# Gate projections of the mLSTM heads by seven block products, with head outputs kept in memory and gate rows made by scans

## The chip, the cores and the metric

The kernel runs on one core of one Trainium2 chip. The metric is the device time of one execution in microseconds (us); less is better. The kernel before takes 914.85 us, the median of three executions (914.61 to 915.66).

## The reference

Two residual layers work on x, 512 rows of 1024 fp32 values. Each computes x + norm(mixer(norm(x))) with a root-mean-square norm on either side. The even layer's mixer has four mLSTM heads (A) and eight stick-breaking attention heads (B); the odd layer's mixer is a trailing-window mean. What matters here, shortened:

```python
u = rmsnorm(x, pre_g) @ w_in                       # 512x1024 @ 1024x9224
qa, ka, va, oa, za, ia, fa, qb, kb, vb, zb = split_cols(u, sizes)
ig, lf = ia + b_i, log_sigmoid(fa + b_f)           # two gates per A head and row
ha = mlstm(silu(conv(qa)), silu(conv(ka)), va, ig, lf)
ya = head_norm(sigmoid(oa) * ha, hn_g) * silu(za)
yb = stick_breaking(qb, kb, vb) * silu(zb)
x = x + rmsnorm(concat([ya, yb]) @ w_out, post_g)  # 512x2048 @ 2048x1024
```

`oa` and `za` are the gate projections of the A heads: 512x1024 times 1024x256 for each head and each of the two. The mLSTM needs, for each head, the running sum of `lf` along the rows and a running maximum of `ig` minus that sum.

## The kernel before

Every fp32 factor of a large product is held as a high and a low part of type fp32r. `split` (L70) makes them: ScalarE copies the value to the high part, VectorE subtracts that to get the low part. `mm3` (L93) then issues three matmuls: high by high, high by low, low by high. `halves` (L86) splits a weight tile, and there are four buffers for the parts (`wh`, `wl`) and two for the fp32 weights (`w32`), which SyncE's DMA queue loads 1 MB at a time (`load`, L78).

`prenorm` (L161) normalises 128 rows, transposes them on TensorE into a bank of PSUM and splits them into `hTh` and `hTl`, the activations with the 1024 features on partitions (eight tiles) and the 512 rows beside. With `keep` (L184) it also stores the fp32 value, which only the second layer uses. `project2` (L196) computes 256 output columns as two groups of 8 x 3 matmuls of 128x512, so 48 matmuls; `raw2` (L350) copies the result out of PSUM (L354).

The even layer runs eight B heads in four pairs (`heads_b`, `stick_pair`, then `raw2` for zb and `close`, L493), then the four A heads in turn: q and k (`project2`, `conv_silu`), v (`values`), the scores `s` and the numerator `num` (`mlstm`, L357), the gates oa and za by `raw2`, and `mlstm_out` (L391). In `mlstm`, the decay weights `w` (ScalarE) are multiplied with the scores on VectorE (L370) and split into `ph` and `pl`, which TensorE multiplies with v. The A heads' gate rows come from `gate_rows` (L248), placed with the third pair: transposes `ips` and `fps`, the logarithm, seven doubling steps for the sum (L277), four transposes into `cps` (L289), seven doubling steps for the maximum, and a store to memory that each head reads back as `bc`.

The head outputs go to `y32` (L101), 32 KB in each partition that lives through the whole kernel. Before it is filled, its space holds the first layer's input tiles (`xt0`, `xs0`, `gain0`) and the gate rows. `out_steps` (L548) walks over the 16 tiles of y in pairs: `y_split`, the out-projection's weights, and 12 matmuls per tile and half of the rows. The first half uses the order `EVEN` (tiles 8 to 15, then 0 to 7), the second `EVEN2`.

The odd layer already uses `strassen2` (L688) for six of its eight z projections. It computes the 1024x256 by 512 product as seven block products instead of eight: sums of weight blocks (`ws`, four VectorE additions), four `halves`, 7 x 4 x 3 = 84 matmuls of 128x256 on sums of activation blocks (`d3`, `d1`, `n2`, `t4`, made by `hidden_sums`, L672), and additions that put the pieces together (`pt`, L715 to L725). Its three PSUM accumulators `psa`, `psb`, `pse` take banks of the tags `pj` (two), `xa` and `xb` (one each). In the A heads `xa` also holds the denominator `den`, and `xb` the mean `mn`.

The program order is not the code's order. A tile framework takes the code as a graph and orders each engine's instructions by a simulated timeline; each engine, and each DMA queue with its issuing engine, then runs its list in order.

Of the kernel before, what the change touches and what calls it, by code (L numbers as in the profile page):

```python
# [36 lines left out]
def body(nc, tc, x, pre_g, post_g, w_in, conv, b_i, b_f, hn_g, w_out, w_in_c, pool_w,  # L37
# [6 lines left out]
    with base as base, psum as psum, dram as dram:  # L44
# [24 lines left out]

        def split(src, hi, lo):  # L70
            A.activation(hi, src, AF.Copy)  # L71
            V.tensor_tensor(lo, src, hi.bitcast(F32), op=ALU.subtract)  # L72
# [28 lines left out]
        y32 = base.tile([P, 16, S], F32, name="y32")  # L101
        yflat = y32.rearrange("p a n -> p (a n)")
        cT = base.tile([P, NB, HA], F32, name="cT")


        xt0 = [yflat[:, i * D:(i + 1) * D] for i in range(4)]
        xs0 = [yflat[:, (4 + i) * D:(5 + i) * D] for i in range(2)]
        gain0 = yflat[:, 6 * D:7 * D]
        xr = x[0].rearrange("(a p) d -> p a d", p=P)
# [51 lines left out]
        def prenorm(xt, xs, tt, gain, name, parts=1, keep=None):  # L161
# [10 lines left out]
            for half in range(2):  # L172
# [10 lines left out]
                if keep is not None:  # L183
                    A.activation(keep[:, half * 4:half * 4 + 4], tp, AF.Copy)  # L184
# [17 lines left out]
        with tc.tile_pool(name="att", bufs=1) as at:  # L202

            def qkt(name): return at.tile([P, S], F32R, tag="qk", bufs=11, name=name)
            def tmp(name): return at.tile([P, S], F32, tag="tmp", bufs=7, name=name)
            def phi(name): return at.tile([P, S], F32R, tag="phi", bufs=4, name=name)
            def plo(name): return at.tile([P, S], F32R, tag="plo", bufs=4, name=name)
            def ozt(name): return at.tile([P, S], F32, tag="oz", bufs=7, name=name)

            def vtile(name):  # L210
                return (at.tile([P, NB, 256], F32R, tag="vh", bufs=2, name=f"vh_{name}"),
                        at.tile([P, NB, 256], F32R, tag="vl", bufs=2, name=f"vl_{name}"))


            v01 = [vtile(f"vb{h}") for h in range(2)]
            w01 = []

            def values01(tt):
                ps = pj(f"psv01_{tt}")
                ts = slice(tt * P, tt * P + P)  # L220
                for k in range(8):
                    wh, wl = w01[k // 2]
                    mm3(ps, (hTh[:, k, ts], hTl[:, k, ts]), (wh[:, k % 2], wl[:, k % 2]),
                        k == 0, k == 7)
                for h in range(2):
                    split(ps[:, 256 * h:256 * h + 256], v01[h][0][:, tt], v01[h][1][:, tt])

            for tt in range(NB):
                prenorm(xt0[tt], xs0[tt % 2], tt, gain0, f"p0{tt}", 1 if tt else 2)
                if tt == 0:  # L230
                    for i in range(2):
                        if i:
                            nc.sync.dma_start(xt0[1], xr[:, 1])
                        w = load(lambda t: [(nc.sync, t[:, 2 * j:2 * j + 2],
                                             w_in[0, 512 * i + 256 * j:512 * i + 256 * j + 256,
                                                  VB:VB + 512]) for j in range(2)], 4, 512, f"v01{i}")
                        w01.extend(halves(w[:, 2 * j:2 * j + 2], f"v01{i}{j}") for j in range(2))
                    for t in range(2, NB):
                        nc.sync.dma_start(xt0[t], xr[:, t])
# [602 lines left out]
```

## Time and profile before

| | us |
|---|---|
| median of three executions | 914.85 |
| the profiled execution | 914.12 |
| its span, first to last instruction | 912.2 |
| ScalarE busy | 485.6 |
| VectorE busy | 570.6 |
| GpSimd busy | 77.3 |

PE is TensorE, DVE is VectorE, ACT is ScalarE, POOL is GpSimd and SP is SyncE, in all rows that follow. Of a row of instruction groups, the name left of the arrow is the tile written, the names right of it are those read; the last numbers are the total busy time, the mean of one in ns, and the idle time before them on the same engine with what ended it. Matmuls are pipelined: one starts long before the one ahead of it ends, so what a matmul costs PE is the distance from its start to the next start, not its listed duration.

### The profile page before, as it was taken

The numbers are of one execution on the slowest core, as the hardware profiler recorded it, in microseconds if no ns is written. First come the engines' busy times: TensorE is split into PE (matmuls) and PEld (weight loads), VectorE is DVE, ScalarE is ACT, GpSimd is POOL, SyncE is SP. The second block draws the span as 40 slices with busy tenths as digits, with TensorE's granted clock in tenths as the row PEclk, the third lists the DMA queues.
The fourth block names the chain that finished last, engine by engine and source line by source line (L and its number), as shares of the span: only waits on it lengthen the run. The fifth ranks groups of instructions, "written<-read, shape, count | busy, mean of one in ns | idle before, by whom it ended". The sixth has DMA issues, their size and how long they took to land.

```text
span 912.2 us, 12027 instructions
## 1 busy us (share of the span) xinstructions
PE 897.8 (98%) x4669; PEld 764.9 (84%) x4669; DVE 570.6 (63%) x847; ACT 485.6 (53%) x814; POOL 77.3 (8%) x221
## 2 busy tenths in 40 slices
PE   7999999999999999999999999999999999999996
PEld 6788889889988888898898887898889898988885
DVE  5435546567876685664775738578484867957442
ACT  6426676766668464564565527574244343455331
POOL 2001101001101201001001000005020110200000
PEclk8999999999999999999999999999999999999999
DMA  8231322222222421333312456623223233146321
GB/s 301 79 107 47 94 71 69 70 70 60 81 93 87 133 93 66 113 94 127 98 49 91 139 185 210 205 93 119 66 92 117 71 127 105 51 160 231 132 96 46
DMA packets 67128, 98.91 MB, mean 108 GB/s; under 512 B 2848, under 2 KB 54136, under 8 KB 67072
## 3 DMA queue, kind: packets, MB, share of 16 engines
q1 hardware_dynamic: 65888, 98.08, 32.7%
q8 instruction: 36, 0.59, 0.2%
q10 hardware_dynamic: 1184, 0.08, 0.1%
q14 instruction: 20, 0.16, 0.1%
HBM read 96.02 MB, written 2.13 MB: 108 GB/s over the span
## 4 chain that ended last, share of the span: by engine, by line
PE 96%; DVE 1%; ACT 1%; DMA 1%; issue 0%; SPq 0%; DVEq 0%; POOL 0%; POOLq 0%; ACTq 0%
PE op L540 10%; PE oq L540 10%; PE ps_qa L97 3%; PE ps_qa L95 3%; PE ps_qa L96 3%; PE ps_p L95 3%; PE ps_p L97 3%; PE ps_p L96 3%; PE psv_va L95 2%; PE psv_va L97 2%; PE psv_va L96 2%; PE ps_zb L95 2%; PE mx L96 2%; PE mx L97 2%; PE mx L95 2%; PE ps_oa L96 2%
## 5 line engine op out<-in xcount | busy, mean ns | idle before, releaser
L95 PE MATMUL ps_p<-hTh,wh_p 128*128 128x512 f32 (+1 forms) x160 | 55.8, 350 | 0.4 <-ACT p L748 0.4
L96 PE MATMUL ps_p<-hTl,wh_p 128*128 128x512 f32 (+1 forms) x160 | 55.9, 350 | 0.2 <-DVE hTl L72 0.2
L97 PE MATMUL ps_p<-hTh,wl_p 128*128 128x512 f32 (+1 forms) x160 | 55.7, 348 | 0.0
L97 PE MATMUL ps_qa<-hTh,wl_qa 128*128 128x512 f32 x128 | 50.3, 393 | 0.0
L95 PE MATMUL ps_qa<-hTh,wh_qa 128*128 128x512 f32 x128 | 50.2, 393 | 0.0
L96 PE MATMUL ps_qa<-hTl,wh_qa 128*128 128x512 f32 x128 | 50.2, 392 | 0.0
L72 DVE TENSOR_TENSOR wl_wo_e<-w_wo_e,wh_wo_e 128x1024 fp32r<-128x1024 f32 x28 | 34.3, 1232 | 23.3 <-ACT wh_wo_e L71 23.2
L71 ACT ACTIVATE wh_wo_e<-w_wo_e 128x1024 fp32r<-128x1024 f32 x28 | 29.4, 1058 | 29.0 <-DMA w_wo_e<-in_w_out_ab 12.3
L71 ACT ACTIVATE wh_p<-w_p 128x1024 fp32r<-128x1024 f32 x16 | 16.9, 1058 | 51.1 <-issue 31.9
L540 PE MATMUL op<-wh_wo_e,yl_e 128*128 128x512 f32 x120 | 39.1, 396 | 0.0
L540 PE MATMUL op<-wl_wo_e,yh_e 128*128 128x512 f32 x120 | 39.1, 396 | 0.0
L540 PE MATMUL op<-wh_wo_e,yh_e 128*128 128x512 f32 x120 | 37.8, 395 | 0.0
L67 ACT ACT_TABLE_LOAD x28 | 35.9, 1283 | 1.3 <-PEq L827 0.8
L97 PE MATMUL psv_va<-wh_va,hTl 128*128 128x256 f32 x128 | 36.1, 282 | 0.0
L95 PE MATMUL psv_va<-wh_va,hTh 128*128 128x256 f32 x128 | 36.1, 282 | 0.0
L96 PE MATMUL psv_va<-wl_va,hTh 128*128 128x256 f32 x128 | 36.1, 282 | 0.0
L320 DVE SCALAR_TENSOR_TENSOR cv<-u,vecs,cv 128x511 f32<-128x511 f32 (+2 forms) x48 | 35.4, 748 | 0.4
L95 PEld LDWEIGHTS ps_p<-hTh,wh_p 128*128 128x128 f32 x160 | 30.1, 189 | 4.7 <-ACT p L748 0.6
L96 PEld LDWEIGHTS ps_p<-hTl,wh_p 128*128 128x128 f32 x160 | 30.2, 189 | 4.3 <-DVE hTl L72 0.4
L97 PEld LDWEIGHTS ps_p<-hTh,wl_p 128*128 128x128 f32 x160 | 30.2, 189 | 4.1
L72 DVE TENSOR_TENSOR wl_wo_o<-w_wo_o,wh_wo_o 128x1024 fp32r<-128x1024 f32 x20 | 24.3, 1223 | 12.5 <-ACT wh_wo_o L71 12.4
L767 POOL TENSOR_TENSOR p<-p,invc 128x1 f32<-128x1 f32 (+3 forms) x16 | 18.4, 1151 | 157.8 <-DVE p L762 157.7
(379 smaller groups left out, 2826.9 us busy)
## 6 DMA issues: line engine op xcount, KB each, us to landing
w_wo_e<-in_w_out_ab SPq DMA_DIRECT2D x14, 1024.0 KB, 4.8
w_wo_o<-in_w_out_c SPq DMA_DIRECT2D x12, 1024.0 KB, 4.8
w_qa<-in_w_in_ab SPq DMA_DIRECT2D x8, 1024.0 KB, 4.9
w_p<-in_w_in_c SPq DMA_DIRECT2D x8, 1024.0 KB, 5.3
w_z<-in_w_in_c SPq DMA_DIRECT2D x8, 1024.0 KB, 5.3
w_qb<-in_w_in_ab SPq DMA_DIRECT2D x4, 1024.0 KB
w_kb<-in_w_in_ab SPq DMA_DIRECT2D x4, 1024.0 KB, 5.2
w_zb<-in_w_in_ab SPq DMA_DIRECT2D x4, 1024.0 KB, 5.1
```

The source lines that it names most:

```text
L67: link(A.preload_act_table_set(TABLE[func]))
L71: A.activation(hi, src, AF.Copy)
L72: V.tensor_tensor(lo, src, hi.bitcast(F32), op=ALU.subtract)
L95: T.matmul(dst, lhsT=ah, rhs=bh, start=first, stop=False, **kw)
L96: T.matmul(dst, lhsT=ah, rhs=bl, start=False, stop=False, **kw)
L97: T.matmul(dst, lhsT=al, rhs=bh, start=False, stop=last, **kw)
L320: V.scalar_tensor_tensor(acc[:, j:], u[:, :S - j], cw(3 - j, c), acc[:, j:], op0=ALU.mult, op1=ALU.add)
L540: T.matmul(ps[a][n], lhsT=l[:, ta], rhs=r[:, 0, n * 512:n * 512 + 512], start=(first and l is yh and r is wh), stop=(last and l is yl))
L767: G.tensor_tensor(sm[:, :e], sm[:, :e], invc[:, :e], op=ALU.mult)
```

## The change

- **Gates.** Each A head's oa and za come from `strassen2` instead of `raw2`: eight calls. `strassen2` now takes its pool and its activation sums; the buffers for `pt` are three instead of four.
- **Activation sums.** The first layer's `prenorm` keeps fp32 transposes (`h32`, eight ScalarE copies of 128x512), and `activation_sums` makes d3, d1, n2, t4 from them (eight VectorE operations of 128x512, four splits of 128x1024) after the first pair's projections; `behind` fixes their place on VectorE.
- **Head outputs.** `close` and `mlstm_out` write their product over z, and GpSimd's DMA queue stores it to `ydr` in memory (16 stores of 256 KB). `out_steps` reads pairs of half tiles back (`yt`, 16 reads of 256 KB on SyncE's queue), one pair ahead. The first pair is read during the last head (`yh_early`); for the second half `soon`, one of the two `w32` buffers, holds two early reads.
- **Gate rows.** Each row of doubling steps becomes four scan instructions of 4x128; the rows take a `bc` buffer and three `oz` tiles. The denominator's floor is computed before the gates (`mlstm_den`).
- **Space.** `y32` exists only in the odd layer; the first layer's input tiles have a pool of their own that closes before the sums' pool opens.

The core of the diff, with the indentation of the moved blocks left as it is in the new file; `strassen2` and the odd layer's `hidden_sums` moved up unchanged but for the arguments and the `part` buffers:

```diff
             wh, wl = (t[:, :a * n].rearrange("p (a n) -> p a n", a=a) for t in (into or whl(name)))
-            split(w, wh, wl)
+            low[name] = split(w, wh, wl)
...
-        y32 = base.tile([P, 16, S], F32, name="y32")
+        ydr = dram.tile([P, 16, S], F32, name="ydr")
...
+        def activation_sums(pool, quarter, tile, order=()):
...
+                for (cs, p), (_, q) in zip(x, y):
+                    if n in ("d3", "d1"):
+                        i = V.tensor_tensor(raw[:, :, cs], p, q, op=ALU.subtract)
+                    else:
+                        i = V.scalar_tensor_tensor(raw[:, :, cs], p, -1.0, q, op0=ALU.mult,
+                                                   op1=ALU.subtract)
+                    if order:
+                        behind(i, order[len(made)])
...
+                split(raw, *hs[n])
...
+        def strassen2(pool, hs, src, name, dsts, silu=False):
...
+            def part(i): return pool.tile([P, 256], F32, tag="part", bufs=3, name=f"pt{i}_{name}")
...
-                prenorm(xt0[tt], xs0[tt % 2], tt, gain0, f"p0{tt}", 1 if tt else 2)
+            prenorm(xt0[tt], xs0[tt % 2], tt, gain0, f"p0{tt}", 1 if tt else 2, h32[tt].__getitem__)
...
-                def scan(buf, op):
-                    cur = 0
-                    for sh in (1, 2, 4, 8, 16, 32, 64):
-                        V.tensor_tensor(buf[1 - cur][:, :, 64:], buf[cur][:, :, 64:],
-                                        buf[cur][:, :, 64 - sh:192 - sh], op=op)
...
+            for B in range(NB):
+                cs = slice(B * P, B * P + P)
+                V.tensor_tensor_scan(b[:, cs], unit, f0[:, cs], 0.0, ALU.mult, ALU.add)
...
+                V.tensor_tensor_scan(mx[:, cs], g[:, cs], g[:, cs], -1e30, ALU.max, ALU.max)
...
-                    V.tensor_tensor(y32[:, c], us[j], z[j], op=ALU.mult)
+                V.tensor_tensor(z[j], us[j], z[j], op=ALU.mult)
+                G.dma_start(ydr[:, c], z[j])
...
-                    V.tensor_tensor(y32[:, 8 + self.h], self.o, z, op=ALU.mult)
+                V.tensor_tensor(z, self.o, z, op=ALU.mult)
+                G.dma_start(ydr[:, 8 + self.h], z)
...
+        def y_back(tile):
+            def src(half, c):
+                t = tile(f"yt{half}{c}").rearrange("p (a n) -> p a n", a=2)
+                nc.sync.dma_start(t, ydr[:, c:c + 2, half * 256:half * 256 + 256])
+                return t
+            return src
...
-                o = raw2(OA + 256 * h, f"oa{h}")
-                z = raw2(ZA + 256 * h, f"za{h}")
-                mlstm_out(h, num, den, bc, o, z)
+            dd = mlstm_den(h, den, bc)
+            o, z = ([ozt(f"r_{n}{h}_{j}") for j in range(2)] for n in ("oa", "za"))
+            if h == HA - 1:
+                ready = y_split(y_back(tmp)(0, EVEN[0]), (qkt("yh_early"), qkt("yl_early")))
+            for t, off, n in ((o, OA, "oa"), (z, ZA, "za")):
+                strassen2(at, hs, w_in[0, :, off + 256 * h:off + 256 * h + 256], f"{n}{h}", t)
+            mlstm_out(h, num, dd, o, z)
...
+        soon = base.tile([P, 8 * WIDE // 4], F32, tag="w32", bufs=2, name="soon")
+        early = [y_back(lambda n, i=i: soon[:, i * S:i * S + S])(1, EVEN2[2 * i]) for i in range(2)]
```

**How the order moves.** Each row is one instruction, or several alike with their count: line, operation, tile written and tiles read, shape. The numbers at the ends of names tell buffers apart.

First place: TensorE in the third A head, between the scores `s` and the numerator `num`. Before, the last scores of the second block are followed by 26 matmuls of the oa projection:

```order
L97 MATMUL s_3917<-h_5_3671,l_5_3756 128x384
L95 MATMUL ps_oa_0_3990<-hTh,wh_oa_0_3991 128x512
L96 MATMUL ps_oa_0_3990<-hTl,wh_oa_0_3991 128x512
...
L95 MATMUL ps_oa_1_4021<-hTh,wh_oa_1_4022 128x512
L96 MATMUL ps_oa_1_4021<-hTl,wh_oa_1_4022 128x512
L95 MATMUL s_3938<-h_4_3630,h_4_3714 128x256
L96 MATMUL s_3938<-l_4_3631,h_4_3714 128x256
L97 MATMUL s_3938<-h_4_3630,l_4_3715 128x256
L95 MATMUL num_3893<-ph_3907,vh_va_3773 128x512
```

Now the same place holds the twelve narrow matmuls of the third and fourth blocks' scores and twelve of the product on `n2`:

```order
L105 MATMUL s_4196<-h_5_3971,l_5_4056 128x512
L105 MATMUL s_4217<-h_5_3971,l_5_4056 128x384
L103 MATMUL s_4238<-h_4_3930,h_4_4014 128x256
...
L105 MATMUL s_4259<-h_5_3971,l_5_4056 128x256
L103 MATMUL psa_oa_4320<-n2h,wh_oa_b 128x256
...
L105 MATMUL psa_oa_4320<-n2h,wl_oa_b 128x256
L103 MATMUL num_4193<-ph_4207,vh_va_4073 128x512
L103 MATMUL num_4194<-ph_4207,vh_va_4073 128x512
L104 MATMUL num_4193<-pl_4208,vh_va_4073 128x512
```

The work between a block's scores and its numerator has become shorter on TensorE.

Second place: VectorE in the gate rows, from the transposed gates `fps` to the four additions (L363) that the transposes into `cps` need. Before:

```order
L263 TENSOR_SCALAR y_65<-fps,gb 4x512
L72 TENSOR_TENSOR vl_vb_2040<-psv_vb_2078,vh_vb_2039 128x256
L271 SCALAR_TENSOR_TENSOR y_65<-y_65 4x4x128
L277 TENSOR_TENSOR y_65<-y_65 4x4x128 x2
L493 TENSOR_TENSOR y_65<-o_1528,r_zb_0_1802 128x512
L277 TENSOR_TENSOR y_65<-y_65 4x4x128
L493 TENSOR_TENSOR y_65<-o_1529,r_zb_1_1833 128x512
```

Now:

```order
L350 TENSOR_SCALAR gr_1897<-fps,gb 4x512
L80 TENSOR_TENSOR vl_vb_2098<-psv_vb_2136,vh_vb_2097 128x256
L354 SCALAR_TENSOR_TENSOR gr_1897<-gr_1897,gr 4x512
L358 SCALAR_TENSOR_TENSOR gr_1899<-ones,gr_1897 4x128 x4
L378 TENSOR_TENSOR tot<-gr_1899 4x1
L360 TENSOR_TENSOR gr_1897<-gr_1898,gr_1899 4x512
L577 TENSOR_TENSOR r_zb_0_1864<-o_1590,r_zb_0_1864 128x512
L577 TENSOR_TENSOR r_zb_1_1895<-o_1591,r_zb_1_1895 128x512
L363 TENSOR_SCALAR gr_1898<-gr_1897,gr_1899 4x128 x4
```

The four scans (L358) stand where the doubling steps began, and on TensorE the `cps` transposes have moved up with them: 67 rows after `fps` instead of 111.

Third place: SyncE's DMA queue at the change from the first half of the out-projection to the second. Before, weights follow weights:

```order
L83 DMA w_wo_e_4945<-in_w_out_ab 128x2x1024
L83 DMA w_wo_e_4983<-in_w_out_ab 128x2x1024
L83 DMA w_wo_e_5171<-in_w_out_ab 128x2x1024
L83 DMA w_wo_e_5209<-in_w_out_ab 128x2x1024
L630 DMA g_post_5026<-in_post_norm_g 128x1024
```

Now:

```order
L637 DMA yt_5455<-ydr 128x2x256
L91 DMA w_wo_e_5421<-in_w_out_ab 128x2x1024
L91 DMA w_wo_e_5461<-in_w_out_ab 128x2x1024
L91 DMA w_wo_e_5501<-in_w_out_ab 128x2x1024
L637 DMA yt_5495<-ydr 128x2x256
L91 DMA w_wo_e_5539<-in_w_out_ab 128x2x1024
L637 DMA soon<-ydr 128x2x256 x2
L91 DMA w_wo_e_5736<-in_w_out_ab 128x2x1024
```

The read `yt_5495` fetches the last A head's output and so stands behind that head's two stores; a weight load, the two reads into `soon` and another weight load stand behind it.

More of the change, by code (lines that the diff above doesn't have):

```diff
@@ L1 @@
+from contextlib import ExitStack
 import concourse.bass as bass
@@ L183, in prenorm @@
                 if keep is not None:
-                    A.activation(keep[:, half * 4:half * 4 + 4], tp, AF.Copy)
+                    A.activation(keep(half), tp, AF.Copy)
         def col_load(src, name):
@@ new lines, in body, with values01 @@
+        v01 = [vtile(f"vb{h}") for h in range(2)]
+        w01, h32 = [], []
+        def values01(tt):
+            ps = pj(f"psv01_{tt}")
+            ts = slice(tt * P, tt * P + P)
+            for k in range(8):
+                wh, wl = w01[k // 2]
+                mm3(ps, (hTh[:, k, ts], hTl[:, k, ts]), (wh[:, k % 2], wl[:, k % 2]),
+                    k == 0, k == 7)
+            for h in range(2):
+                low["v01"] = split(ps[:, 256 * h:256 * h + 256], v01[h][0][:, tt], v01[h][1][:, tt])
@@ new lines, in stick_pair, with first, second @@
+        def stick_pair(pair, tags):
+            def first(si, t):
+                for s, tag in zip(pair, t):
+                    s.scores(si, tag)
+                for s in pair:
+                    s.soft_exp(si)
+                for s in pair:
+                    s.soft_ln(si)
+            def second(si):
+                for s in pair:
+                    s.sums(si)
+                for s in pair:
+                    s.weigh(si)
+            for si in range(NB - 1, -1, -1):
+                first(si, tags[si % 2])
+                if si < NB - 1:
+                    second(si + 1)
+            second(0)
@@ new lines, in out_tile @@
+        def out_tile(steps, ps, a):
+            ends = steps[-1][2]
+            for group in ([(s, (n,)) for n in range(2) for s in steps] if ends else
+                          [(s, (0, 1)) for s in steps]):
+                ((wh, wl), (yh, yl), last, first), ns = group
+                ta = slice(a * P, a * P + P)
+                for l, r in ((yh, wh), (yh, wl), (yl, wh)):
+                    for n in ns:
+                        T.matmul(ps[a][n], lhsT=l[:, ta], rhs=r[:, 0, n * 512:n * 512 + 512],
+                                 start=(first and l is yh and r is wh), stop=(last and l is yl))
@@ L638, in ytiles, with back @@
                         od.tile([P, S], F32R, tag="plo", bufs=5, name=f"yl_{n}"))
-            ready = y_split(1, EVEN2[0], ytiles("first"), "e")
+            load_y = y_back(lambda n: od.tile([P, S], F32, tag="sz", bufs=4, name=n))
+            def back(half, c): return early[1] if c == EVEN2[2] else load_y(half, c)
+            ready = y_split(early[0], ytiles("first"))
             xn = od.tile([P, NB, D], F32, name="xn")
+            y32 = od.tile([P, 16, S], F32, name="y32")
             gpo, gpr = gains(post_g[0], "g_post0"), gains(pre_g[1], "g_pre1")
```

813 lines of the change are left out of this document (392 added, 421 removed).

## The prediction

> **What bounds the kernel now.** I read the page's busy times first, then the chain that ended last, then what TensorE waited for, then windows of single stages. All rows are of the profile of before.
>
> ```profile
> span 912.2 us, 12027 instructions
> PE 897.8 (98%) x4669; PEld 764.9 (84%) x4669; DVE 570.6 (63%) x847; ACT 485.6 (53%) x814; POOL 77.3 (8%) x221
> PE 96%; DVE 1%; ACT 1%; DMA 1%; issue 0%; SPq 0%; DVEq 0%; POOL 0%; POOLq 0%; ACTq 0%
> PE tp_p L179 <- DVE y L174: 3.2, 1, 3.2
> PE warm L119 <- POOL ident masks.py:199: 1.6, 1, 1.6
> PE op L540 <- POOL p L740: 0.8, 1, 0.8
> ```
>
> TensorE is busy for 98% of the span and carries 96% of the chain. Its longest waits (total, times, longest) are 3.2 and 1.6 us, both in the opening; the next is 0.8 us. The windows (length; busy us of PE, PEld, DVE, ACT, POOL with counts; granted clock; DMA share; GB/s) say where the slack of the others lies:
>
> ```profile
> 0.00:30.00 30.00, 24.75 (x111) 19.77 (x112) 16.97 (x29) 17.14 (x31) 5.13 (x37) 0.89 0.65 229
> 30.00:60.00 30.00, 30.00 (x134) 24.52 (x133) 12.59 (x15) 10.88 (x15) 0.00 (x0) 1.00 0.33 106
> 410.00:470.00 60.00, 60.00 (x310) 51.27 (x309) 38.62 (x53) 31.07 (x48) 4.00 (x9) 1.00 0.31 104
> 680.00:740.00 60.00, 60.00 (x370) 53.70 (x369) 42.94 (x59) 26.02 (x41) 7.62 (x24) 1.00 0.33 106
> ```
>
> 410 to 470 is most of an A head: TensorE full, VectorE 64%. 680 to 740 is the odd layer with three calls of the seven-product form: TensorE full too, VectorE at 72%. So the kernel ends when TensorE has worked off its list, and a change counts by the matmuls it removes and by the waits it brings.
>
> **The change part by part.** First the price of a matmul, by the distance of starts:
>
> ```profile
> 409.93 0.39 PE L95 MATMUL ps_oa<-hTh,wh_oa 128*128 128x512 f32 x1
> 415.96 0.28 PE L95 MATMUL s<-h,h 128*128 128x256 f32 x1
> 689.72 0.28 PE L96 MATMUL psa_z<-n2l,wh_z_b 128*128 128x256 f32 x1
> 694.24 0.40 PE L95 MATMUL mx<-pph,wh_pw 128*128 128x512 f32 x1
> ```
>
> From 409.93 to 415.96 stand 26 matmuls of 128x512: 6.03 / 26 = 0.232 us each. From 689.72 to 694.24 stand 38 of 128x256, of four products: 4.52 / 38 = 0.119 us each. A projection was 48 x 0.232 = 11.13 us and becomes 84 x 0.119 = 9.99 us. It saves 1.14 us, and eight of them **9.1 us**. The other matmul groups keep their shapes and counts.
>
> *VectorE and ScalarE in an A head.* The new work has its rows in the odd layer, with the same shapes:
>
> ```profile
> L72 DVE TENSOR_TENSOR wl_oa<-w_oa,wh_oa 128x1024 fp32r<-128x1024 f32 x8 | 9.8, 1223 | 6.5 <-ACT wh_oa L71 6.5
> L72 DVE TENSOR_TENSOR wl_z_c<-ws_z,wh_z_c 128x1024 fp32r<-128x1024 f32 x6 | 7.3, 1222 | 2.2 <-ACT wh_z_c L71 1.6 <-PE psa_z L97 0.5
> L72 DVE TENSOR_TENSOR wl_z_d<-w_z,wh_z_d 128x512 fp32r<-128x512 f32 x6 | 4.1, 687 | 0.1
> L696 DVE TENSOR_TENSOR ws_z<-w_z 128x512 f32<-128x512 f32 x6 | 4.2, 692 | 15.0 <-DMA w_z<-in_w_in_c 15.0
> L725 DVE TENSOR_TENSOR sz<-pse_z,pt_z 128x256 f32<-128x256 f32 x6 | 2.5, 422 | 10.6 <-PE pse_z L97 10.6
> L71 ACT ACTIVATE wh_oa<-w_oa 128x1024 fp32r<-128x1024 f32 x8 | 8.5, 1062 | 16.5 <-PE ps_qa L96 16.5
> L715 ACT ACTIVATE pt_z<-psa_z 128x256 f32<-128x256 f32 x6 | 2.3, 376 | 0.5 <-PE psa_z L97 0.3
> L354 ACT ACTIVATE r_oa<-ps_oa 128x512 f32<-128x512 f32 x8 | 4.6, 579 | 0.0
> ```
>
> A call adds on VectorE four weight sums (4 x 0.69), one whole and one half low part more (1.22 + 0.69) and three pieces (3 x 0.42): 5.9 us, so 11.9 us in a head with two calls. ScalarE gets 1.5 high parts (1.6) and four copies of 128x256 (1.5) and loses two of 128x512 (1.2): +1.9 us a call. The window of 410 to 470 says 38.6 of 60, so 41.5 us of VectorE in a head of 64.4. With the new work it is at most 53.4 us in a head of 64.4 - 2.3 = 62.1: 86%. That is below TensorE, but the cover of each single chain shrinks. The shortest is the one from scores to numerator that the order shows:
>
> ```profile
> 410.25 1.15 DVE L370 SCALAR_TENSOR_TENSOR w<-s,w 128x512 f32<-128x512 f32 x2
> 411.32 1.22 DVE L72 TENSOR_TENSOR wl_za<-w_za,wh_za 128x1024 fp32r<-128x1024 f32 x1
> 412.45 0.69 DVE L72 TENSOR_TENSOR pl<-w,ph 128x512 fp32r<-128x512 f32 x1
> 417.38 0.39 PE L96 MATMUL num<-pl,vh_va 128*128 128x512 f32 x1
> ```
>
> Before, `pl` was ready at 413.14 and TensorE wanted it at 417.38: 4.2 us to spare. Now TensorE has, from the start of the first block's last score to the first `num` on `pl`: one matmul of 128x512, one of 128x384 (0.17), 24 of 128x256 and two `num` of 128x512, so 0.23 + 0.17 + 2.86 + 0.46 = 3.7 us. The chain needs 0.4 us until that score has ended, the 2.9 us that it took before from `w` to the end of `pl`, and 0.3 us more for the rows that now stand between (a value part, one more `w`, half a weight part: about 1.5 us where 1.1 stood): 3.6 to 4.2 us. The wait is 0 to 0.5 us a head. I take 0.25, so **+1.0 us** for four heads. What queues behind it: `num` heads TensorE's list, so all of TensorE waits.
>
> *Gate rows.* After the change the transposes into `cps` stand about 8.2 us of matmuls behind `fps` (before about 18), and VectorE must have finished by then:
>
> ```profile
> 212.83 0.27 PE L261 MATMUL fps<-ident,gates 128*4 128x128 f32 x1
> 216.75 0.68 DVE L271 SCALAR_TENSOR_TENSOR y<-y 4x512 f32<-4x512 f32 x1
> L277 DVE TENSOR_TENSOR y<-y 4x512 f32<-4x512 f32 x14 | 9.4, 675 | 0.2
> L286 DVE TENSOR_SCALAR y<-y 4x128 f32<-4x128 f32 x4 | 0.9, 270 | 0.0
> L412 DVE RECIPROCAL dd<-dd 128x512 f32<-128x512 f32 x4 | 13.4, 3354 | 2.1 <-ACT dd L68 2.1
> ```
>
> From `fps` to the end of L271 before the sums: 217.43 - 212.83 = 4.6 us. Behind it come four scans, a tiny addition (0.1), one operation of 4x512 (0.6), two head products (1.2) and four additions of 4x128 (0.9): 7.4 us and four scans. No scan stands in the trace. By the additions of 4x128 one costs 0.22 us in a row, by an operation that does one element at a time like the reciprocal 3354 / 4 = 0.84 us. So cps is ready 8.3 to 10.8 us after `fps`, a wait of 0.1 to 2.6 us, once. I take 0.3 us for a scan, nearest the row of its own shape: **+0.4 us**. The VectorE time saved is about 14 x 0.6 - 8 x 0.3 = 6 us, beside full matmuls, and worth nothing.
>
> *Opening.*
>
> ```profile
> L184 ACT ACTIVATE y<-tp_p 128x512 f32<-128x512 f32 x8 | 4.7, 593 | 2.0 <-DVE hTl L72 2.0
> ```
>
> Eight more such copies are 4.7 us of ScalarE while TensorE waits for ScalarE's high parts now and then. ScalarE has 12.9 us free of the first 30, and in the order most copies stand behind the value parts that TensorE needs. Bounds 0 and 0.7 us (one copy late at one tile, on the first wait); I take **+0.2**. The activation sums (about 10 us of VectorE, 4.2 of ScalarE) lie in 30 to 60, where VectorE is busy for 12.6 of 30 us and ScalarE for 10.9: nothing, unless the stick's first weights come late.
>
> *Head outputs.* A store on GpSimd's queue isn't in the trace. The nearest rows are SyncE's (size and us from issue to landing):
>
> ```profile
> out<-xo SPq DMA_DIRECT2D x8, 256.0 KB, 2.0
> y<-in_x SPq DMA_DIRECT2D x2, 256.0 KB, 3.1
> ```
>
> So 2.0 to 3.1 us a trip, 4 to 6.2 for store and read. All heads but the last have tens of us for it. For the last head: its product follows about 13 us after `mn` (a reciprocal of 3.35, then four operations of 0.69 behind other rows), so with trip and split (0.6 + 0.7) y is ready about 20 to 25 us behind `mn`, and TensorE has 11.3 of the out-projection's tiles to do between `mn` and that y, 12 matmuls each: 11.3 x 12 x 0.232 = 31 us. Cover is 6 us or more; gone, each us of delay is one of TensorE. The other queues: `yt_5495` holds up a weight load and the reads into `soon` behind it on SyncE's queue for as long; the second half begins with four held tiles' weights (4 x 2.8 = 11 us), which cover a load. Bounds 0 and 3 us; I take **+0.3** for the change of layers, where TensorE waited 0.8 us already. The z tiles now stay taken until their store has landed; the next head's convolution takes them about 1.7 us behind that by the same rows, so no term.
>
> [...]
>
> **The sum.** -9.1 + 1.0 + 0.4 + 0.2 + 0.3 = -7.2 us. From the profiled execution's 914.12 that is 906.9. The median, 914.85, lies 0.7 above that execution, so I predict **907.6 us** for the median.
>
> **The rivals.**
>
> *No wait at all.* Every chain fits, as in 680 to 740 where TensorE stays full: 914.85 - 9.1 = 905.7 us. For it: TensorE lost almost nothing outside the opening before. Against: covers of 0 to 0.5 us where there were 4.2.
>
> *VectorE becomes the bound in the A heads*, the slower side. Engines work off their lists in order, so idle time behind a wait can't always be filled. VectorE idled 64.4 - 41.5 = 22.9 us a head before; 62.1 - 53.4 = 8.7 are left. If more than 8.7 us of the old idle time was forced (a `num` wants `pl`, `pl` wants `w`, the second head product wants the reciprocal), each us above lengthens the head. At half of it, 11.5 us, a head loses 2.8 us, four 11.2: 914.85 - 9.1 + 11.2 + 0.9 (the small terms) = 917.9 us. It is slower by over 0.2% from about 2.5 us a head, and it eats half the gain at 1.1. For it: 86% is higher than any stage that the trace shows. Against: 72% in 680 to 740 costs TensorE nothing, and the low parts are made well ahead of their matmuls. With 1 to 2 us a head the time is 911 to 915 us.
>
> *The trip through memory is late.* If the store takes 10 us where I put 2 to 3, cover turns into a wait of 2 to 4 us at the out-projection, and the held queue adds up to 3: 910 to 914 us. For it: a kind of DMA that the trace does not show. Against: 2.0 to 3.1 us for the same size on the queue that it does show.
>
> *The product form does not pay here.* `psb` and `den` share one bank, `pse` and `mn` another, so products could stand in line for banks, which the odd layer does not do. A bank comes free with one copy of 0.38 to 0.58 us, and the lists put 12 or more other matmuls (1.4 us) between: I count it with the terms of VectorE.
>
> **How the numbers follow.** Chances: the forecast with waits of 1 to 4 us, 906 to 910 us, 0.5; no wait, 905 to 906, 0.2; VectorE partly or the trip late, 910 to 913, 0.12; within 0.2% (1.8 us, about what a measurement of this kernel can tell from no change), 913 to 916.7, 0.08; slower by VectorE, 0.1. So faster 0.82, same 0.08, slower 0.1. The range reaches from no wait with a spread of the runs, 904.8, to 912.5; it takes in the upper ends of gates and trip together and leaves the VectorE case above it.
>
> **What would show it.** Right: starts 0.119 us apart in the A heads' `psa_oa`, a window over an A head with TensorE full but for under 0.6 us, head to head about 62 us instead of 64.4; waits of `num` on `pl` and of `cps` on VectorE of some tenths each; store rows landing within 3 us. Wrong: TensorE waiting on VectorE's low parts or pieces by over 1 us a head, a wait of `op` on `yh_e` near the end of the first half, or `cps` waiting over 2 us. A scan dearer than 0.84 us, a store dearer than 10 us, or forced idle time of VectorE would make the prediction wrong.

## The result, and the profile after

| | before | changed |
|---|---|---|
| median of five executions, us | 914.71 (914.55 to 915.66) | 909.24 (908.98 to 910.29) |
| profiled execution, us | 914.12 | 910.0 |
| its span, us | 912.2 | 908.3 |

The changed kernel takes 0.9943 of the time of before, 95% interval 0.9932 to 0.9954: 5.5 us less, where 7.2 were forecast from the profiled execution. The time lies in the predicted range. In a second comparison the same kernel gave 0.9948 (0.9934 to 0.9961), so the gain is some 4 to 6 us.

The page of the changed kernel, busy times and shares of the chain that ended last:

```profile
span 908.3 us, 12851 instructions
PE 892.1 (98%) x4957; PEld 772.9 (85%) x4957; DVE 614.1 (68%) x925; ACT 507.3 (56%) x858; POOL 88.7 (10%) x233
PE 97%; DVE 1%; ACT 1%; DMA 1%; issue 0%; DVEq 0%; SPq 0%; POOL 0%; POOLq 0%; ACTq 0%
```

TensorE has 288 matmuls more, 8 x (84 - 48) as the change says, and is still what ends the kernel. What it waited for (total us, times, longest), of the changed kernel:

```profile
PE s L103 <- DVE w L450: 2.6, 4, 0.7
PE tp_p L189 <- DVE xs L184: 2.1, 1, 2.1
...
PE psb_oa L103 <- ACT dd L473: 0.7, 1, 0.7
PE psb_za L103 <- DVE r_oa L275: 0.5, 1, 0.5
```

Two of these rows are new against before: `psb_oa` on `dd` and `psb_za` on `r_oa` (both in the first A head). A third, `s` on `w`, now comes once in each A head; before, it stood among TensorE's waits once, in the second head:

```profile
PE s L95 <- DVE w L370: 0.2, 1, 0.2
```

In the changed kernel no `num` waits for `pl` by more than 0.2 us, no `op` for `yh_e`, and the transposes into `cps` are not among these rows. The windows of the changed kernel for the opening and one A head:

```profile
0.00:30.00 30.00, 26.07 (x112) 20.71 (x113) 16.38 (x28) 19.59 (x36) 3.96 (x33) 0.89 0.65 229
30.00:60.00 30.00, 29.98 (x134) 24.05 (x133) 22.27 (x28) 16.15 (x22) 0.00 (x0) 1.00 0.33 106
410.00:470.00 60.00, 59.32 (x390) 54.31 (x389) 48.37 (x70) 35.59 (x59) 6.50 (x11) 1.00 0.35 112
```

In the head TensorE lost 0.7 of 60 us where it lost nothing before, and VectorE went from 38.6 to 48.4 us (81%). From 30 to 60 VectorE's busy time rose by 9.7 us, the activation sums, and TensorE stayed full.

The same can be had for the whole trace. I took the distance between the starts of neighbouring matmuls and subtracted the plain step of the first one's shape (0.232 us for 128x512, 0.175 for 128x384, 0.119 for 128x256; the few other shapes by a step of their own, which can move the first two rows by some tenths, alike in both columns). What is left is time that TensorE did not spend on matmuls:

| us lost on TensorE, by start distance | before | changed |
|---|---|---|
| opening, 0 to 50 | 9.0 | 8.9 |
| 50 to 275 (stick heads, gate rows) | 0.0 | -0.1 |
| A heads, 275 to 500 | -0.3 | 5.3 |
| out-projection and change of layers, 500 to 625 | 3.5 | 3.7 |
| odd layer | 0.5 | 0.4 |
| sum | 12.6 | 18.2 |

So 9.1 us of matmuls are saved, as forecast, and 5.6 lost in the A heads; 3.5 are left, against 3.9 between the two spans; the stretch behind the last matmul is 0.5 shorter (7.0 instead of 7.6). (The medians say 5.5: the profiled execution of the changed kernel is 0.8 above its own median, that of before 0.6 below.) Everything else together is within 0.2 us. The question is what takes 5.6 us in the heads, where the prediction put 1.0.

The timeline of the changed kernel's third A head shows it (start, us, engine and line, operation, tiles; in brackets the idle time before it and what ended it). First TensorE:

```profile
410.13 0.57 PE L105 MATMUL s<-h,l 128*128 128x512 f32 x2
...
411.35 0.58 PE L105 MATMUL s<-h,l 128*128 128x512 f32 x2
412.61 0.39 PE L103 MATMUL s<-h,h 128*128 128x256 f32 x1 [0.68 <-DVE w L450]
...
414.13 0.31 PE L103 MATMUL psa_oa<-n2h,wh_oa_b 128*128 128x256 f32 x1
```

Then VectorE at the same place:

```profile
411.87 1.16 DVE L450 SCALAR_TENSOR_TENSOR w<-s,w 128x512 f32<-128x512 f32 x2 [1.80 <-PE s L105]
414.76 3.06 DVE L80 TENSOR_TENSOR pl<-w,ph 128x512 fp32r<-128x512 f32 x4
```

The scores have two banks of PSUM. Blocks 1 and 2 fill them by 411.35; block 3 (128x256, 412.61) needs the first bank back, and that is free only after VectorE has multiplied it with the decay weights. VectorE was not late: it had waited 1.80 us for the last score. The multiplication starts 0.13 us after that matmul's end (411.35 + about 0.39), takes 0.69, and TensorE goes on 0.05 later. (The row 411.35 holds two matmuls, the last of block 1 and the last of block 2.) Between the last of block 1 and the first of block 3 stands only that one of block 2 (0.18 us), so TensorE loses 0.85 us by start distance. The bracket says 0.68, since a matmul counts as busy to its listed end, past the point where the next could have started. Before, 26 matmuls of the oa projection stood there. In the second head of before, though, only the last four matmuls of block 2 stood there (0.70 us), and its row above is the wait that came of it, 0.32 us by start distance: the trace of before already showed this wait, in small.

### The profile page after: what moved, and what is told of

Same layout as the page of the kernel before. It is cut to its first block, busy times and chain, and to the rows that moved or that the text cites. A ratio compares the mean times of both kernels' runs of the same rounds, so it can differ in the third digit from the quotient of the medians.

```text
span 908.3 us, 12851 instructions
## 1 busy us (share of the span) xinstructions
PE 892.1 (98%) x4957; PEld 772.9 (85%) x4957; DVE 614.1 (68%) x925; ACT 507.3 (56%) x858; POOL 88.7 (10%) x233
## 4 chain that ended last, share of the span: by engine, by line
PE 97%; DVE 1%; ACT 1%; DMA 1%; issue 0%; DVEq 0%; SPq 0%; POOL 0%; POOLq 0%; ACTq 0%
PE op L625 10%; PE oq L625 10%; PE ps_qa L103 3%; PE ps_qa L104 3%; PE ps_qa L105 3%; PE ps_p L103 3%; PE ps_p L105 3%; PE ps_p L104 3%; PE psv_va L103 2%; PE psv_va L105 2%; PE psv_va L104 2%; PE ps_zb L103 2%; PE mx L105 2%; PE mx L103 2%; PE mx L104 2%; PE ps_zb L105 2%
## 5 line engine op out<-in xcount | busy, mean ns | idle before, releaser
L625 PE MATMUL op<-wl_wo_e,yh_e 128*128 128x512 f32 x112 | 36.0, 396 | 0.0
L625 PE MATMUL op<-wh_wo_e,yl_e 128*128 128x512 f32 x112 | 36.0, 396 | 0.0
L625 PE MATMUL op<-wh_wo_e,yh_e 128*128 128x512 f32 x112 | 35.2, 397 | 0.0
```

The source lines that it names most:

```text
L625: T.matmul(ps[a][n], lhsT=l[:, ta], rhs=r[:, 0, n * 512:n * 512 + 512], start=(first and l is yh and r is wh), stop=(last and l is yl))
```

## The experiments

Two theories were tested. The first: the **bank round trip** in the heads is what the change pays for, and other matmuls between blocks 1 and 3 would take it away. The rival: **VectorE and ScalarE are short of time** in the heads, so that a wait filled in one place comes back in another. In all that follows "the lost time of the heads" is the row of 275 to 500 above, got in the same way.

**1. The gates wide again, all else as changed.** oa and za by the 48 wide matmuls:

```diff
-            o, z = ([ozt(f"r_{n}{h}_{j}") for j in range(2)] for n in ("oa", "za"))
...
-            for t, off, n in ((o, OA, "oa"), (z, ZA, "za")):
-                strassen2(at, hs, w_in[0, :, off + 256 * h:off + 256 * h + 256], f"{n}{h}", t)
+            o = raw2(OA + 256 * h, f"oa{h}")
+            z = raw2(ZA + 256 * h, f"za{h}")
```

> The changed kernel with oa and za of all heads by the wide projections again (48 matmuls of 128x512 each), all else as changed; the activation sums are still made but not used. Theory: the other parts of the change (copies and sums in the opening, scans, head outputs through memory) neither cost nor gain, and the long filler is back: no wait of s on w, 914.7 with 0.5 either way. Rival: they cost (the trip, the sums): 915.5 or more; or they gain (shorter gate rows, opening): 914 or less.

Measured: 913.70 us, 0.9995 of before (0.9986 to 1.0004). No wait stands in the heads, whose lost time is -0.5 us. The median lies 1.0 us below that of the kernel before beside it, which the rival had put down to a gain (914 or less), but the interval reaches from 1.3 us less to 0.4 us more, and by start distance the two kernels lose the same in sum. So the gate rows, the activation sums in the opening and the trip of the outputs through memory together cost or gain nothing that can be told from zero, and within that the change of time is that of the product form: its matmuls and its waits.

**2. Only za in products**, oa wide:

> The changed kernel with only oa by the wide projections again; za stays in products. Theory (bank): four calls save 4 x 1.14 = 4.6 us, and oa's 24 wide matmuls stand between the scores again, so nothing waits there: 914.7 - 4.6 = 910.1. Rival (VectorE load): half of the added VectorE work stays, and with it about half of the heads' waits of 5 us: 912.5.

Measured: 911.56 us, 0.9970 (0.9960 to 0.9980), between the two forecasts. No `s` waits: wide oa matmuls stand between the blocks again, as before the change. The heads lose 0.6 us. But the first tiles of the out-projection now wait for the weights' parts, as these rows of that kernel's waits show:

```profile
PE op L625 <- DVE wl_wo_e L80: 0.7, 1, 0.7
PE op L625 <- ACT wh_wo_e L79: 0.3, 1, 0.3
```

Half the products should have brought 4.6 us, and 2.1 came against the kernel of experiment 1. By start distance the heads took 1.1 and the out-projection 1.7 of it. So the waits at the bank go when oa is wide, even with narrow products in za, but the rival has something too: with the new work in the last head, VectorE and ScalarE are late with the parts that follow it.

**3. Fill the gap with the product on `n2`.** In heads 2 to 4 TensorE's order was fixed so that block 3 of the scores stands behind the 12 matmuls of that product (1.4 us). `pin` fixes the order of two matmuls; the lines that mark them are left out here:

```diff
+            if h:
+                pin(f"s{h}2", f"oa{h}_n2")
             mlstm_out(h, num, dd, o, z)
```

> The changed kernel with one edit: in the second, third and fourth A head the third block's scores are ordered behind the oa product on n2 (twelve matmuls of 128x256, 1.43 us), which the changed kernel runs after them. Theory (bank): scores wait because the two banks for scores are full until VectorE has read the first one, 0.85 us a head with nothing between; twelve matmuls cover it. The three waits of s on w go, no other comes, 3 x 0.85 = 2.5 us less than the changed kernel's 909.2: 906.7. Rival (VectorE is the bound there): its rows, not the order on TensorE, set the pace; the wait moves to num on ph or pl, and the time stays 908.5 to 909.5.

Measured: 916.01 us, 1.0016 (1.0006 to 1.0026), slower than before the change. The waits of this kernel:

```profile
PE psa_oa L103 <- ACT pt_oa L279: 6.3, 3, 2.1
...
PE s L103 <- DVE w L456: 0.6, 1, 0.6
```

The three waits of 0.85 us on `w` went, and three of 2.27 (by start distance) on `pt_oa` came. The matmuls chosen as filler could not run: the product on `n2` adds to the bank `psa_oa`, and the first product in it must be copied out before. ScalarE's list, here from the third head, shows why that copy is late:

```profile
409.83 1.28 ACT L69 ACT_TABLE_LOAD   x1
411.13 1.93 ACT L70 ACTIVATE w<-bc,cT 128x512 f32<-128x512 f32 x4
413.07 1.28 ACT L69 ACT_TABLE_LOAD   x1
414.36 0.38 ACT L79 ACTIVATE vh_va<-psv_va 128x256 fp32r<-128x256 f32 x1
414.64 0.62 ACT L79 ACTIVATE wh_oa_d<-w_oa 128x512 fp32r<-128x512 f32 x1
415.16 0.38 ACT L279 ACTIVATE pt_oa<-psa_oa 128x256 f32<-128x256 f32 x1
```

The copy stands behind the four exponentials of the decay weights with a table load on each side, and two high parts: 5.3 us of ScalarE without a pause. Neither theory's numbers came; both had overlooked this second bank. It may also be why the framework's planner had left the gap open: of the products, the next in line was not ready. (The row left on `w` is head 1, whose order was not touched. A further kernel, which fixed the first head's products as well, gave no time: in that order instructions would have waited for each other without end.)

**4. The copy on VectorE.** So the first copy of each product call in the even layer goes to VectorE, which is idle there, and the order is left to the planner:

```diff
-            A.activation(t1, pa, AF.Copy)
+            if silu:
+                A.activation(t1, pa, AF.Copy)
+            else:
+                V.tensor_copy(t1, pa)
```

> The changed kernel with one line changed: in the A heads the first product is copied out of its bank (the first pt) by VectorE and not by ScalarE. ScalarE came to that copy only behind four exponentials, two table loads and a weight part, and the product on n2, which adds to the same bank, had to wait for it. In the new order twelve matmuls on n2 stand between the scores of the first and the third block in heads 2 to 4 (1.6 us where 0.2 stood), and more in head 1. Theory (bank, with ScalarE's list behind it): between the last score of the first block and the first of the third, TensorE needs about 1.0 us of other matmuls (0.18 + 0.85 and 0.29 + 0.72 in the changed kernel); now it has 1.6. The waits of s go, and the one behind den; the one between the second products of oa and za (0.7) stays: 909.2 - 2.5 - 0.7 - 0.9 = 905.1. Rival (VectorE is the bound in the heads): eight more copies on it, no gain or 909.5 and more.

Measured: 909.76 us, 0.9946 (0.9933 to 0.9958). The 905.1 of the theory was missed, and the time is the rival's: no gain over the changed kernel. Yet the planner now puts products between the blocks by itself, and all waits on `w` and on `dd` are gone. In their place this kernel has:

```profile
PE psb_za L103 <- DVE r_oa L278: 1.2, 1, 1.2
...
PE psa_za L105 <- DVE wl_za_a L80: 0.8, 1, 0.8
PE psa_za L103 <- ACT wh_za_a L79: 0.6, 1, 0.6
PE num L104 <- DVE pl L80: 0.5, 3, 0.2
```

Heads 2 to 4 lose 0.3 us each where they lost 0.9, `num` on `pl` among it, the wait that the prediction had put there (0.31 to 0.33 us a head by start distance). The first head loses 3.7 us instead of 2.7. Its `v` is computed before it begins (the code's `if h`), so it has fewer matmuls of its own beside the parts that VectorE and ScalarE make; that this is the reason was not tried.

**5. The order of the code.** The oa product is written ahead of the mLSTM, so that the planner meets it earlier:

```diff
+            o, z = ([ozt(f"r_{n}{h}_{j}") for j in range(2)] for n in ("oa", "za"))
+            strassen2(at, hs, w_in[0, :, OA + 256 * h:OA + 256 * h + 256], f"oa{h}", o)
             num, den = mlstm(h, q, k, v, bc)
...
-            for t, off, n in ((o, OA, "oa"), (z, ZA, "za")):
-                strassen2(at, hs, w_in[0, :, off + 256 * h:off + 256 * h + 256], f"{n}{h}", t)
+            strassen2(at, hs, w_in[0, :, ZA + 256 * h:ZA + 256 * h + 256], f"za{h}", z)
```

> The changed kernel with oa's products written ahead of the head's scores in the code, za's behind as before. The order then puts 3.0, 0.7, 1.6 and 0.5 us of other matmuls between the scores of the first and the third block of heads 1 to 4, and two us and more behind each den. Theory (bank): with 1.0 us needed, waits of 0, 0.3, 0, 0.5 are left of the 4.8 us in the heads: 909.2 - 4.0 = 905.2. Rival (VectorE's load): as the load is the same, the waits come back elsewhere: 908 or more.

Measured: 910.77 us, 0.9963 (0.9949 to 0.9976): no better than the changed kernel, and on the rival's side of the two forecasts. Its waits:

```profile
PE op L625 <- DVE wl_wo_e L80: 1.3, 1, 1.3
...
PE ps_qa L105 <- DVE wl_qa L80: 0.5, 1, 0.5
PE op L625 <- ACT wh_wo_e L79: 0.5, 1, 0.5
PE s L103 <- DVE w L450: 0.5, 2, 0.3
```

The heads lose 3.9 us instead of 5.3, the out-projection 6.1 instead of 3.7. Two `s` waits are left, of 0.32 and 0.49 us by start distance, with 0.70 and 0.53 us of other matmuls in their gaps, as the theory had said; what it had not said is what came elsewhere.

**6. Both edits**, of 4 and 5:

> Both edits of the two runs before. Between the scores of the first and the third block stand 3.2, 1.6, 2.1 and 2.1 us, behind each den 2.3 us and more, and the second products of oa and za are far apart. Theory (bank): no wait over 0.3 us is left in the A heads, the eight products give their whole 9.1 us: 914.7 - 9.1 = 905.6 by the time of before, 909.2 - 4.8 = 904.4 by that of the changed kernel. Rival: 907 or more.

Measured: 908.18 us, 0.9931 (0.9919 to 0.9944). No wait on `w`, none on `dd`; the heads lose 1.9 us. The 904.4 to 905.6 of the theory was missed, the rival's 907 or more came: the heads' loss did not go to zero, and the out-projection now loses 5.1 us instead of 3.7. The waits:

```profile
PE psa_za L105 <- DVE wl_za_a L80: 0.7, 2, 0.4
PE op L628 <- ACT wh_wo_e L79: 0.6, 1, 0.6
...
PE op L628 <- DVE wl_wo_e L80: 0.4, 1, 0.4
```

On VectorE the low part for the out-projection, `wl_wo_e`, stands behind the last head's work, its reciprocal of 3.35 us included.

**7. The changed kernel and the kernel of experiment 6 (version 6) again, side by side**, with two more kernels on the same chip:

> The changed kernel as it is, on the same chip as the three that follow, so that they can be compared with it: 5.3 us under the kernel before (909.2 against 914.5), with 4.8 us of waits in the A heads.

> The kernel with both edits (oa's products ahead of the scores in the code, first copy on VectorE) once more beside the changed kernel. By the distances of TensorE's starts 1.9 us of waits in the A heads and 1.3 more at the out-projection stand against 5.3 and 0 in the changed kernel: 2 us faster than it. If waits in the heads are only pushed to later stages: no difference.

Measured: 909.95 us, 0.9948 (0.9934 to 0.9961), for the changed kernel, and 908.77, 0.9935 (0.9922 to 0.9947), for version 6. Version 6 is the fastest kernel here that computes all of the reference. It is 1.2 us below the changed kernel, less than the 2 expected. The intervals against before overlap, but each of its five times (908.1 to 909.3) is under each of the changed kernel's five (909.4 to 910.8) on the same chip, and it led in the first comparison too.

**8. The first head's wait, pinned away.** In kernel 4, the second za product of the first head (`psb_za`) is moved behind the oa product on `t4`, and the first one behind that on `n2`:

```diff
+            if h == 0:
+                pin("za0_11", "oa0_n2")
+                pin("za0_21", "oa0_t4")
```

> The kernel with the first copy on VectorE, and in the first A head the oa product on t4 ordered between the second products of oa and za, which share a bank (1.4 us between them where nothing stood and 1.4 us were waited). Theory (bank): that wait goes, 1.4 us less than without it (909.8): 908.4, and 3.3 us of waits are left in the A heads. Rival (VectorE frees the bank late because it has too much to do): it comes back as a wait on another part.

Measured: 909.98 us, 0.9948 (0.9936 to 0.9961), as kernel 4; the 908.4 of the theory was missed. Its waits, where 1.2 us of `psb_za` on `r_oa` stood:

```profile
PE psa_oa L103 <- DVE r_oa L290: 1.5, 1, 1.5
```

The wait moved to another bank that VectorE frees, as the rival had said. But VectorE did not have too much to do there, as its timeline shows:

```profile
299.85 0.69 DVE L483 TENSOR_TENSOR dd<-dd,bc 128x512 f32<-128x512 f32 x1 [3.71 <-ACT dd L482]
301.26 1.23 DVE L80 TENSOR_TENSOR wl_za_c<-ws_za,wh_za_c 128x1024 fp32r<-128x1024 f32 x1 [0.72 <-ACT wh_za_c L79]
302.40 0.42 DVE L284 TENSOR_TENSOR r_oa<-psb_oa,pt_oa 128x256 f32<-128x256 f32 x1
302.73 0.41 DVE L290 SCALAR_TENSOR_TENSOR r_oa<-psa_oa,pt_oa 128x256 f32<-128x256 f32 x1
```

It stood idle for 3.71 and 0.72 us just before. The two pieces that free the banks stand in its list behind the low part `wl_za_c`, and this waits for the high part, which ScalarE makes from 300.16 on. So in this kernel the order of VectorE's list holds both banks, whichever TensorE asks for first. What another order would give was not tried.

**9. Take work off VectorE.** The reciprocal of 128x512 in each A head is left out, and what it would have inverted is used as it stands; 13.4 us of VectorE are gone:

```diff
             act(dd, dd, AF.Sqrt)
-            V.reciprocal(dd, dd)
```

> The changed kernel without the reciprocal in the A heads (its input is used as it is): VectorE has 3.35 us less to do in each head. The order shifts with it: 0.3, 1.6, 0.7, 0.7 us of other matmuls stand between the scores of the first and the third block. Theory (bank, 1.0 us needed): waits of s of 0.7, 0, 0.3, 0.3 us, and the first head's two other waits (1.5) stay: 2.8 of 5.3, so 2.5 under the changed kernel. Rival (VectorE's load sets the pace): all waits in the heads go, 4.8 or more under the changed kernel.

Measured: 907.78 us, 0.9924 (0.9912 to 0.9937), 2.2 us below the changed kernel beside it, near the 2.5 expected from the bank and far from the rival's 4.8 or more. Its waits:

```profile
PE s L103 <- DVE w L450: 0.7, 2, 0.6
PE psb_oa L103 <- ACT dd L473: 0.7, 1, 0.7
PE psb_za L103 <- DVE r_oa L275: 0.5, 1, 0.5
```

The waits of the first head are what they were. This run can't tell why, since that head's reciprocal comes behind them (at 318 us in the changed kernel, the waits at 289 to 302); but the rows of the changed kernel can: VectorE had idled 1.06 us when it came to `psb_oa`, ScalarE 2.22 when it came to `den`. Of the `s` waits, head 2's is gone and those of heads 3 and 4 are 0.32 and 0.31 us, with 0.70 us of other matmuls in the gap: with less on VectorE the planner had ordered TensorE's list differently. (The row gives idle time and lists only two; the sums here are start distances.) So this is not a pure test of load.

All kernels, the one before included, give one rule for the gap between block 1's last score and block 3's first:

| kernel and head | other matmuls in the gap, us | wait by start distance, us | sum |
|---|---|---|---|
| before, head 2 | 0.70 | 0.32 | 1.02 |
| changed, heads 2 to 4 | 0.18 | 0.85 | 1.03 |
| changed, head 1 | 0.29 | 0.72 | 1.01 |
| experiment 5, two heads | 0.70 and 0.53 | 0.32 and 0.49 | 1.02 and 1.02 |
| experiment 9, heads 3 and 4 | 0.70 | 0.32 and 0.31 | 1.02 and 1.01 |
| experiments 1, 2, 4, 6 | 1.6 and more | 0 | |

The round trip of the bank takes 1.02 us of TensorE's time, and matmuls that stand in it are free. In each row with a wait VectorE had stood idle before the multiplication (1.8 to 5.1 us), so these waits are not of its load; what the trip takes when VectorE comes late is not shown.

**10. How much cover the trip through memory has.** The last head's two stores are issued four times each, in one execution:

```diff
-                G.dma_start(ydr[:, c], z[j])
+                for _ in range(4 if h == HA - 1 else 1):
+                    G.dma_start(ydr[:, c], z[j])
```

> The changed kernel with each of the two stores of the last A head issued four times, one behind the other. Theory (cover): the last y tiles are split about 6 us before TensorE wants them; three more stores of about 3 us make them 9 us late, so TensorE waits about 3 us for them near the end of the first half of the out-projection, and 912 or so comes out. Rival (no cover): over 8 us; rival (stores to one place don't queue): nothing, 909.2.

Measured: 918.53 us. That is the time of the rival without cover (over 8 us more than the changed kernel) and not the 912 of the theory, but the traces show that the cover is there. In the changed kernel, GpSimd and ScalarE at the last head's store and split:

```profile
519.90 0.54 POOL L501 DMA_DIRECT2D ydr<-r_za  x1 [0.87 <-issue]
531.51 0.62 ACT L79 ACTIVATE yh_e<-yt 128x512 fp32r<-128x512 f32 x1
```

With the repeated stores, the last issue on GpSimd and the split on ScalarE, and then TensorE's wait:

```profile
535.85 1.18 POOL L502 DMA_DIRECT2D ydr<-r_za  x2 [3.21 <-DMA ydr<-r_za]
544.13 0.63 ACT L79 ACTIVATE yh_e<-yt 128x512 fp32r<-128x512 f32 x1 [7.21 <-DMA yt<-ydr]
```

```profile
PE op L626 <- ACT yh_e L79: 5.0, 1, 5.0
```

The split came 544.13 - 531.51 = 12.6 us later, some 11.5 with this trace's own shift taken off, and TensorE waited 5.0. So the changed kernel has about 6 us to spare here, the prediction's figure; what is later than that, TensorE waits for. Its own trace says the same: the split ends at 532.13, and TensorE's first matmul on it starts at 538.61. The forecast went wrong in two places. The repeated stores hold the read up by more than the 9 us that it gave them: it is issued at 539.03 instead of 524.36, 13.5 us later without the shift. And the wait costs more than its 5.0 us: the matmuls behind it ran at a granted clock of 0.50 up to 549.4, 0.43 us apart instead of 0.23, which is another 2.2 us. Of the 8.5 us between the two spans, 1.1 lie in the opening, which differs by as much between kernels that have it alike.

## Why the prediction was right, and where it was not

- **Matmuls, -9.1: right.** The starts lie 0.119 us apart in the heads' products too (408.71 to 408.83 and on), and lost time apart what is left of the span's change is this amount. Experiment 1 against the changed kernel: 3.5 us between the spans, where 9.1 less the heads' 5.8 is 3.3.
- **Heads, +1.0: the term that was mis-sized; it is 5.6.** The prediction found the right stretch, from scores to numerator, and the right reason, that TensorE's work between them had become short. But it followed the chain forward, from `s` over `w` to `pl` and `num`, and put 0.25 us a head there. That wait did not come in the changed kernel, where the larger one ahead of it hides it; with that gone, in experiment 4, it was 0.31 to 0.33 us a head, within the forecast's 0 to 0.5. (The rows of the chain add up to 3.6 us; for the upper end of 4.2 no rows are given. It took 4.1, from 411.35 to the end of the first `pl` at 415.44.) The prediction overlooked that the same `w` also gives the bank back to block 3's scores, which come earlier in TensorE's list than `num`. Its own quoted order shows the two blocks' scores one behind the other; it counted them as cover when they were what had to wait. That is 0.72 + 3 x 0.85 = 3.3 us. The first head's shared bank is another 0.85 + 0.68 = 1.5: the rows say `den` is read into `dd` by ScalarE before `psb_oa` may start, and then `psb_oa` by VectorE before `psb_za`. The rival "the product form does not pay here" had named this bank, and had dismissed it since 12 other matmuls would stand between; in head 1 none did. The trace of before had one wait of `s` on `w`, too, which was not followed up. The remaining 0.8 is spread over many small distances and was not followed.
- **VectorE as the bound: half right.** VectorE came to 81% of the head's window, below the "at most 86%", and the waits at the scores' bank come with VectorE idle, so they are not of its load. But the order of its list and of ScalarE's is a second limit: in experiments 2, 4, 5, 6 and 8 a filled gap came back in part as a wait for `wl_za_a`, `r_oa` or the out-projection's weight parts, and the rival's times came in 4, 5 and 6. Version 6 in experiment 7 loses 3.4 us less in the heads than the changed kernel beside it, but 1.6 more in the out-projection, and so gets 1.2 us and not the 5 that the heads lose.
- **Gate rows, +0.4: right in size of its parts, and the wait was 0.1.** The scan, for which the trace of before had no row, was put at 0.3 us. From VectorE's timeline of the changed kernel:

```profile
217.40 1.36 DVE L358 TENSOR_TENSOR_SCAN gr<-ones,gr 4x128 f32<-4x128 f32 x4
```

  Four in a row take 1.36 us, 0.32 from start to start. The transposes' wait vanished in the next row of matmuls; 50 to 275 lost nothing.
- **Opening, +0.2: 0 within what can be told.** The opening's longest wait (`tp_p` on `xs`) is between 1.4 and 2.7 us in these kernels, whose openings are the same. A difference of 0.2 can't be seen beside that.
- **Out-projection and memory, +0.3: measured +0.2.** In the median a store took what SyncE's rows had suggested, 2.0 to 3.1 us; the last head's two, on which the term rests, took 5.2 and 4.4, beside weight loads (the DMA engines were busy for 0.96 of that time), and the cover took that in. The DMA issues of the changed kernel (count, size, median us from issue to landing):

```profile
yt<-ydr SPq DMA_DIRECT2D x14, 256.0 KB, 5.0
ydr<-r_zb POOLq DMA_DIRECT2D x8, 256.0 KB, 2.4
ydr<-r_za POOLq DMA_DIRECT2D x8, 256.0 KB, 2.9
soon<-ydr SPq DMA_DIRECT2D x2, 256.0 KB, 2.8
```

  The rival of the late trip is out: the cover was 6 us as worked out, and TensorE waited for no `yh_e`. In the A heads a cast of VectorE beside a store does not show in its time: six stores had one cast (0.43 us) beside them and took 2.5 to 3.0 us, and the slowest, the last head's 5.2, had none. Two stores of the last B pair had two casts beside them and took 3.8 and 5.0, beside weight loads as well; no run takes these apart.

By the start distances of the two profiled executions the sum was 3.7 us too good (-7.2 against -3.5): 4.6 too little for the heads, 0.9 too much for the other terms. Against the medians it was 1.7 too good, since these lie further apart (5.5 us) than the profiled pair (4.1), as far as single executions scatter. The range held because its upper end had room for waits of 1 us a head and more, and 5.6 / 4 = 1.4 is what came. That the time also fell into the band of 906 to 910 is luck in part: the band stood for waits of 1 to 4 us, and the heads alone lost 5.6, in a place that the forecast did not have. Two of its signs of being right failed, if narrowly: the window over an A head lost 0.68 us (under 0.6 was forecast), and from head to head it is 63.2 us (about 62).

## What to carry to other kernels

When work is taken out from between two steps, look at every buffer that the steps in between give back, not only at the chain of values: the next user of a PSUM bank may stand earlier in the list than the next user of the result. A small wait in the trace of before, in the one place where the gap was already short, gives the price. Before filling such a gap, ask of each candidate which bank it needs itself and who frees that. A wait that is filled by a new order can return in part elsewhere: where the engines that feed TensorE have the least slack, or where a step that frees a bank stands late in their lists. So the gain is known only after a run.

## What the runs showed of the hardware

- **A wait of 2.3 us can cost more than itself.** In experiment 3 the three waits are alike (2.09, 2.11 and 2.11 us idle in their rows), but only behind the one in the third head the matmuls ran at half pace for about 3 us. The windows of that kernel (granted clock is the third number from the end) around this wait (1.93 us of the first row without a matmul) and behind it:

```profile
412.00:415.41 3.41, 1.48 (x8) 1.01 (x6) 1.69 (x4) 3.38 (x7) 0.00 (x0) 1.00 0.00 0
415.50:418.00 2.50, 2.41 (x11) 2.41 (x12) 1.65 (x3) 0.97 (x3) 1.07 (x1) 0.50 0.30 62
418.00:420.00 2.00, 2.00 (x15) 1.95 (x15) 0.57 (x1) 1.60 (x3) 0.11 (x1) 0.80 1.06 370
```

  The start distance is 0.21 us there instead of 0.119, about 1.5 us lost in addition. Behind the second head's wait and the fourth's the starts lie 0.12 us apart from the second matmul on (from 351.26 and from 481.81). Why one of three waits was followed by the lower clock and the other two were not, these runs do not show. The waits of 0.85 us in the changed kernel left the clock at 1.00.
- **Stores to one place followed each other one by one.** GpSimd needed 0.54 to 0.57 us to issue a store of 256 KB in the A heads. Issued again to the same place, each pair waited for the one before: the issues of experiment 10 lie 4.3, 6.1 and 4.4 us apart. Whether the chip asks for that, or the order that the framework gives to writes to one place, the rows do not say.
- **Most reads back took longer than the stores.** 256 KB into `yt` took 5.0 us in the median where the stores took 2.4 and 2.9, but the two reads into `soon` took 2.8; the reads share SyncE's queue and the DMA engines with weight loads of 1 MB, which was not taken apart.
